# HGRN level scores: two chunks of tokens on one 128-column stationary tile

## The chip, the core and the metric

The kernel runs on one core of one Trainium2 chip. The metric is the device time of one execution, in microseconds. The engines meant below: TensorE (PE; PEld is its load of stationary operands), VectorE (DVE), ScalarE (ACT), GpSimd (POOL) and SyncE (SP), which issues most of the transfers. They run side by side, each through its own list of instructions in order, and wait for one another by semaphores.

## The reference

One decoder layer, float32, on 512 tokens of width 1024: a half-step SwiGLU FFN (hidden width 2816), a token mixer, and a second half-step FFN, each between two RMS norms. The mixer projects the normed input with one matrix and splits the columns among four HGRN2 heads (hq, hf, hi, hgate, 128 columns a head each) and four mLSTM heads. The change touches the HGRN2 heads:

```python
    """S_t = diag(f_t) S_{t-1} + k_t v_t^T (k_t = 1 - f_t), o_t = S_t^T q_t.
...
        G = jnp.cumsum(gc, axis=2)
        o_inter = jnp.einsum("bhtk,bhkv->bhtv", qc * jnp.exp(G), S)
        rel = G[:, :, :, None, :] - G[:, :, None, :, :]
        decay = jnp.exp(jnp.where(causal, rel, -jnp.inf))
        scores = jnp.sum(qc[:, :, :, None, :] * kc[:, :, None, :, :] * decay, axis=-1)
        o = o_inter + jnp.einsum("bhts,bhsv->bhtv", scores, vc)
```

The score of query t and key s (s not after t) is the sum over a head's 128 columns of q[t] k[s] exp(G[t] - G[s]), where G is the running sum of the logarithms of the forget gates. The exponent differs per column, so the factor cannot simply be split between q and k: exp(-G[s]) alone could overflow.

## The kernel before

**Stages.** The program does FFN1, then the mixer (about 340 to 600 us of the span), then FFN2. Weights come by SyncE (raw), are split by ScalarE (a rounded part, L294) and VectorE (the rest, L296) into two parts of a reduced format, and each projection is three matmuls of parts (L198 to L200 with the input as stationary operand, L549, L560 and L619 with the weight). Activations are split the same way into the tiles xq, one for each 256 tokens and 512 input columns: L370 on ScalarE and L371 on VectorE, behind transposes L364 on TensorE.

**Scores by levels.** Kernel chunks are 128 tokens, so there are 4 chunks and 16 pairs of head and chunk. Scores of a chunk are computed in seven levels, LEVELS = (1, 64, 32, 16, 8, 4, 2), and a diagonal. At level c the tokens are cut into blocks of 2c; queries of a block's second half meet keys of its first half, with the G at the end of the first half as reference, so both exponents are at most 0: qe = q exp(G - ref) on 64 queries of each chunk (L1421, L1423, L1428), and ke = exp(ref - kk), where kk holds G - ln k by then (L1422, L1424). Only first-half columns of a ke tile (128x2x512) are written, the others keep what they have; both ke tiles are first filled with a copy of kk (L1806). TensorE multiplies all columns up to the last used key: `rows(c)` is 72, 96, 112, 120, 124, 126 for c = 64 to 2. One matmul for each of the 8 pairs of a pass (a pass p is two heads) has these key columns stationary and 64 query columns moving (L1440). The result is (keys x queries), of which most pairs belong to no common block; a copy under a mask (L1445, `copy_predicated`, masks by L1314 and L1316 on GpSimd) puts the right ones into sT, the transposed scores. Level 1 is one matmul with ones (L1435); the diagonal is one of 128x128 by 128 for each head and chunk, L1486, copied under the mask eye (L1488). So in the kernel before

```python
            k8, q8 = flat(ke).rearrange("p (n s) -> p n s", s=P), qe.rearrange("p (n u) -> p n u", u=64)
            r = self.rows(c)
            for m in range(8):
                nc.tensor.matmul(sc[:r, 64 * m : 64 * m + 64], k8[:, m, :r], q8[:, m], start=True, stop=True)
```

The levels go two by two: `hgrn_levels` issues a pair's vector work, then `fill(n)`, n steps of projection matmuls from a list of jobs, and then the pair's matmuls in one group. There are three groups a pass, six in all. The jobs are hq, conv, rows, hi (the HGRN values, `job_t`, chunk of tokens stationary), mv (the mLSTM values, into vm), later hg and mo. `hgrn_decays` (L1374 to L1391) makes the decays of keys to the chunk's end (ek, L1389), which `hgrn_edges` transposes (L1401) into kdt for the state updates (L1498, with vh, the values of hi).

**Order.** The code is written in an order of dependence and filler steps, and a scheduler sorts each engine's instructions again before the program is built; which instruction stands where is therefore told below from the built programs. GpSimd makes the masks, then the sums f2sums over FFN2's output weights (L944, transfers that add, each waiting for the one before), then the memset of C (L1651) and the causal masks on the mLSTM's e (L1614). An mLSTM head's e comes from neg_m (L1588) over L1610 to L1614; L1624 multiplies it with the score of L1622 and frees their banks of PSUM. SyncE loads the gains of norms into two tiles of 1024 columns, gpre and gpost (L165), and graw, the weights of the gates' rows (L1515).

Of the kernel before, what the change touches and what calls it, by code (L numbers as in the profile page):

```python
# [8 lines left out]
F32 = mybir.dt.float32  # L9
# [114 lines left out]
class Layer:  # L124
# [1027 lines left out]
    def t_mm(self, ps, w, k, kk, i):  # L1152
        s = (i * P, (i + 1) * P)
        self.mm3(ps, self.xop(k, 0, *s), self.xop(k, 1, *s), w[:, 0, kk, :], w[:, 1, kk, :], k == 0, k == ND - 1)

    def job_t(self, name, then):

        acc = [self.ps() for _ in range(NT)]
        for k2 in range(ND // 2):
# [3 lines left out]
            for i in range(NT):  # L1163
                for kk in range(2):
                    self.t_mm(acc[i], w, 2 * k2 + kk, kk, i)
                    if kk == 0:
                        yield
# [137 lines left out]
    def masks(self, mc, mb):  # L1305
# [3 lines left out]
        self.mask = mb.tile([P, len(LEVELS), 64], I32, name="mask")  # L1309
        nc.gpsimd.memset(self.mask, 1)  # L1310
        for n, c in enumerate(LEVELS):
            m = self.mask[:, n, :].rearrange("p (b c) -> p b c", c=c)
            pat = [[-2 * c, 64 // c], [0, c]]
            nc.gpsimd.affine_select(m, m, pattern=pat, compare_op=ALU.is_ge, fill=0.0, base=0, channel_multiplier=1)  # L1314
            pat = [[2 * c, 64 // c], [0, c]]
            nc.gpsimd.affine_select(m, m, pattern=pat, compare_op=ALU.is_ge, fill=0.0, base=c - 1, channel_multiplier=-1)  # L1316
        self.eye = mb.tile([P, P], I32, name="eye")
        nc.gpsimd.memset(self.eye, 1)
        nc.gpsimd.affine_select(
            self.eye, self.eye, pattern=[[1, P]], compare_op=ALU.is_equal, fill=0.0, base=0, channel_multiplier=-1  # L1320
        )
# [51 lines left out]
    def hgrn_decays(self, p):  # L1373
# [15 lines left out]
        nc.vector.tensor_tensor(chunks(d), end.broadcast_to([P, 8, P]), chunks(H), op=ALU.subtract)  # L1389
# [14 lines left out]
    def rows(self, c):  # L1404

        return P if c == 1 else max(P - c, 72)

    def hgrn_level(self, p, n, ke):
# [4 lines left out]
        flat = lambda t: t.rearrange("p a t -> p (a t)")  # L1413
        blk = lambda t: flat(t).rearrange("p (b two c) -> p b two c", two=2, c=c)
        qe = self.st("qe")
        qe3 = qe.rearrange("p (b c) -> p b c", c=c)
        if c > 1:
            el = self.st("el")
            el3 = el.rearrange("p (b c) -> p b c", c=c)
            ref = blk(G)[:, :, 0, c - 1 : c].broadcast_to([P, 512 // c, c])  # L1420
            nc.vector.tensor_tensor(qe3, blk(G)[:, :, 1, :], ref, op=ALU.subtract)  # L1421
            nc.vector.tensor_tensor(el3, ref, blk(kk)[:, :, 0, :], op=ALU.subtract)  # L1422
            nc.scalar.activation(qe, qe, AF.Exp)  # L1423
            nc.scalar.activation(blk(ke)[:, :, 0, :], el3, AF.Exp)  # L1424
# [9 lines left out]
        if c == 1:  # L1434
            nc.tensor.matmul(sc, self.one.broadcast_to([P, P]), qe, start=True, stop=True)  # L1435
        else:
            k8, q8 = flat(ke).rearrange("p (n s) -> p n s", s=P), qe.rearrange("p (n u) -> p n u", u=64)
            r = self.rows(c)
            for m in range(8):
                nc.tensor.matmul(sc[:r, 64 * m : 64 * m + 64], k8[:, m, :r], q8[:, m], start=True, stop=True)  # L1440
        yield
        r = self.rows(c)
        so = self.sT[:, 8 * p : 8 * p + 8, :].rearrange("p n (b two c) -> p n b two c", two=2, c=c)[:, :, :, 1, :]
        mk = self.mask[:, n : n + 1, :].broadcast_to([P, 8, 64]).rearrange("p n (b c) -> p n b c", c=c)
        nc.vector.copy_predicated(so[:r], mk[:r], sc.rearrange("p (n b c) -> p n b c", n=8, c=c)[:r])  # L1445
# [34 lines left out]
    def hgrn_diag(self, p):  # L1480
        nc = self.nc
        for a in range(2):
            sc = self.ps()
            for c in range(NT):
                s = slice(c * P, (c + 1) * P)
                nc.tensor.matmul(sc[:, s], self.kk[p][:, a, s], self.q[p][:, a, s], start=True, stop=True)  # L1486
            h = 2 * p + a
            nc.vector.copy_predicated(  # L1488
                self.sT[:, 4 * h : 4 * h + 4, :], self.eye[:, None, :].broadcast_to([P, NT, P]), sc.rearrange("p (n s) -> p n s", s=P)
# [101 lines left out]
    def conv(self, n, ps):  # L1591
# [3 lines left out]
        nc.scalar.copy(x, ps)  # L1595
# [375 lines left out]
```

## Time and profile before

| | us |
|---|---|
| median of 3 runs | 928.69 |
| lowest and highest run | 927.12, 928.71 |
| profiled execution: its span | 926.8 |
| TensorE busy | 918.0 |
| VectorE, ScalarE, GpSimd busy | 765.4, 523.9, 184.0 |

The page gives no time of the profiled execution apart from its span, so the span stands for it. A row of a group gives line, engine, operation, output and inputs, shapes and count, then busy time and the mean of one in ns, then the idle time of the engine ahead of these instructions and who ended it. A row of the timeline gives start and length in us; instructions in sequence from one line are put together with their count, and an idle time ahead stands in brackets. A row of windows gives length, busy time and records of the engine, its granted clock, the transfer engines' share and rate. A matmul on plain float32 tiles leaves two records: the 8 of L1440 for one level and pass stand as 16.

### The profile page before, as it was taken

Reading aid. Unit: us, or ns where it says so; the run is one execution under the profiler, and the core shown is the slowest. Engines: PE = TensorE matmul, PEld = TensorE weight load, DVE = VectorE, ACT = ScalarE, POOL = GpSimd, SP = SyncE. Lnnn points to the kernel's source line nnn. Section 1 sums busy time; section 2 is a strip of 40 time slices with the busy share of each in tenths; the row PEclk is TensorE's granted clock in tenths of the full one; section 3 lists DMA queues with packets and bytes.
Section 4 is the critical chain, followed back from the end, with each engine's and each line's share of the span. In section 5 each row is a group of like instructions: output and inputs, shape, how many; then the busy total and the mean of one; then the engine's idle time right before and its main releaser. Section 6 shows DMA issues by size and latency. Waiting matters only on the chain.

```text
span 926.8 us, 18311 instructions
## 1 busy us (share of the span) xinstructions
PE 918.0 (99%) x7428; PEld 885.5 (96%) x7428; DVE 765.4 (83%) x993; ACT 523.9 (57%) x751; POOL 184.0 (20%) x252
## 2 busy tenths in 40 slices
PE   9999999999999999999999999999999999999997
PEld 8999999999999999998888887899999999999997
DVE  6899988889887877698757565799898989998886
ACT  7645455557566466956533345595454545756661
POOL 2531112111111045552230310314000000010002
PEclk9999999999999999999999999999999999999999
DMA  9354778766897925899742124352354435278542
GB/s 313 76 175 122 187 202 204 193 149 160 224 274 227 254 70 138 168 193 189 156 91 70 46 92 153 97 183 68 116 160 137 136 116 159 93 230 247 172 148 92
DMA packets 123384, 145.42 MB, mean 157 GB/s; under 512 B 12066, under 2 KB 96034, under 8 KB 123300
## 3 DMA queue, kind: packets, MB, share of 16 engines
q1 hardware_dynamic: 107332, 129.05, 45.7%
q0 software_dynamic: 15680, 14.69, 12.1%
q8 instruction: 58, 0.95, 0.4%
q10 hardware_dynamic: 288, 0.52, 0.2%
q14 instruction: 26, 0.21, 0.1%
HBM read 142.14 MB, written 31.46 MB: 187 GB/s over the span
## 4 chain that ended last, share of the span: by engine, by line
PE 63%; ACT 0%; DVE 0%; DVEq 0%; POOLq 0%; issue 0%; POOL 0%; ACTq 0%
PE ps L619 23%; PE ps L1012 8%; PE ps L549 6%; PE ps L198 5%; PE ps L200 5%; PE ps L199 5%; PE ps L1004 4%; PE ps L1440 2%; PE ps L560 1%; PE ps L364 1%; PE ps L1533 0%; PE ps L1738 0%; PE ps L1711 0%; PE ps L1486 0%; PE ps L1735 0%; PE ps L1498 0%
## 5 line engine op out<-in xcount | busy, mean ns | idle before, releaser
L294 ACT CAST w<-raw 128x1024 fp32r<-128x1024 f32 x246 | 250.9, 1028 | 196.1 <-PE ps L619 79.2
L296 DVE TENSOR_TENSOR w<-raw,w 128x1024 fp32r<-128x1024 f32 x246 | 299.2, 1220 | 31.2 <-ACT w L294 29.9
L619 PE MATMUL ps<-xq,w 128*128 128x256 f32 x2016 | 237.3, 277 | 0.0
L619 PEld LDWEIGHTS ps<-xq,w 128*128 128x128 f32 x2016 | 233.3, 188 | 0.0
L619 PE MATMUL ps<-sq,w 128*128 128x256 f32 x1512 | 178.4, 277 | 0.0
L619 PEld LDWEIGHTS ps<-sq,w 128*128 128x128 f32 x1512 | 174.9, 188 | 0.0
L310 DVE TENSOR_TENSOR raw<-raw,raw 128x1024 f32<-128x1024 f32 x72 | 89.7, 1250 | 7.7 <-DMA raw<-in_ffn_w_in_dram 6.4
L1012 PE MATMUL ps<-w,hs 128*128 128x256 f32 x672 | 80.9, 276 | 0.0
L1004 PE MATMUL ps<-w,hs 128*128 128x256 f32 x672 | 79.2, 276 | 0.0
L1012 PEld LDWEIGHTS ps<-w,hs 128*128 128x128 f32 x672 | 78.3, 188 | 0.0
L198 PE MATMUL ps<-w,xq 128*128 128x512 f32 x192 | 77.9, 407 | 0.1
L1004 PEld LDWEIGHTS ps<-w,hs 128*128 128x128 f32 x672 | 77.5, 188 | 0.0
L199 PE MATMUL ps<-w,xq 128*128 128x512 f32 x192 | 74.8, 391 | 0.0
L200 PE MATMUL ps<-w,xq 128*128 128x512 f32 x192 | 74.8, 391 | 0.0
L549 PE MATMUL ps<-xq,w 128*128 128x256 f32 x480 | 55.7, 277 | 0.0
L549 PEld LDWEIGHTS ps<-xq,w 128*128 128x128 f32 x480 | 54.9, 188 | 0.5 <-issue 0.5
L944 POOL DMA_DIRECT2D f2sums<-in_ffn_w_out_dram x15 | 20.2, 1492 | 176.4 <-DMA f2sums<-in_ffn_w_out_dram 176.1
L884 ACT CAST hs<-hf 128x1024 fp32r<-128x1024 f32 x32 | 33.7, 1053 | 28.0 <-PE ps L1012 20.3
L885 DVE TENSOR_TENSOR hs<-hf,hs 128x1024 fp32r<-128x1024 f32 x32 | 39.1, 1221 | 9.0 <-ACT hs L884 8.4
L944 POOL DMA_DIRECT2D f1sums<-f1sums x26 | 23.1, 889 | 106.3 <-DMA f1sums<-in_ffn_w_out_dram 55.4
L198 PEld LDWEIGHTS ps<-w,xq 128*128 128x128 f32 x192 | 36.1, 188 | 8.5 <-issue 1.0
L200 PEld LDWEIGHTS ps<-w,xq 128*128 128x128 f32 x192 | 36.0, 188 | 8.1 <-DVE xq L371 0.3
(272 smaller groups left out, 1216.8 us busy)
## 6 DMA issues: line engine op xcount, KB each, us to landing
raw<-in_ffn_w_in_dram SPq DMA_DIRECT2D x98, 512.0 KB, 4.6
raw<-in_ffn_w_out_dram SPq DMA_DIRECT2D x44, 512.0 KB, 4.8
raw<-in_w_mix_in_dram SPq DMA_DIRECT2D x28, 512.0 KB, 6.8
raw<-f2sums SPq DMA_DIRECT2D x15, 512.0 KB, 4.4
raw<-f1sums SPq DMA_DIRECT2D x13, 512.0 KB, 6.0
raw<-in_w_mix_out_dram SPq DMA_DIRECT2D x8, 512.0 KB, 3.8
f2sums<-in_ffn_w_out_dram SPq DMA_DIRECT2D x30, 128.0 KB, 5.2
f2sums<-in_ffn_w_out_dram SPq DMA_DIRECT2D x15, 256.0 KB, 5.7
```

Of the source, the lines that this page charges most:

```text
L198: mm(ps, sh, mh, start=start, stop=False, **kw)
L199: mm(ps, sh, ml, start=False, stop=False, **kw)
L200: mm(ps, sl, mh, start=False, stop=stop, **kw)
L294: nc.scalar.copy(hi, raw)
L296: self.low = nc.vector.tensor_tensor(lo, raw, hi.bitcast(F32), op=ALU.subtract)
L310: added = (nc.vector if late else nc.gpsimd).tensor_tensor(o, o, c, op=ALU.add)
L549: mm(ps[:, u0:u1], w[:, a, k, :], self.xop(k, b, u0, u1), start=k + n + m == 0, stop=k == ND - 1 and n == 2, skip_group_check=True,)
L619: self.nc.tensor.matmul(ps[:, c], wb[b][:, k, v], left[d][:, k, :], start=first and a + n + k == 0, stop=n == 2 and k == KH - 1, skip_grou ...
L885: self.nc.vector.tensor_tensor(lo, src, hi.bitcast(F32), op=ALU.subtract)
L944: nc.gpsimd.dma_start(to[:, a:b], v, accum_op=ALU.add)
L1004: mm(out, a[kk][:, i * P : (i + 1) * P], w[:, b, kk, QUARTER * v : QUARTER * (v + 1)], start=begin and c == kk == n == 0, stop=kk == 1 and ...
L1012: mm(ps[:, QUARTER * c : QUARTER * (c + 1)], A[a][:, c], B[b], start=begin and c == n == 0, stop=n == 2, skip_group_check=True,)
```

## The change

Keys of two neighbouring chunks are put on one stationary tile. At each level the even chunk's used keys lie in first halves of blocks; the odd chunk's tokens are written in reversed order, so that its first halves fall on the columns of the second halves. Both together fill 128 columns, none unused. One matmul has these 128 columns stationary and the 64 queries of both chunks, 128 columns, moving; a pass has 4 of them at a level instead of 8. Its result has four blocks (even or odd keys by even or odd queries), of which the mask takes two. The rows of odd chunks in sT then stand in reversed token order, and everything that is contracted with them too: the diagonal's keys (new copies kr on ScalarE, L1495 of the changed program), ek, and the HGRN values, which `hi` computes from a reversed copy of the input (`turned_x`, four ScalarE copies of 128x1024, L1161). The copies for the first 256 tokens take the tiles of gpre and gpost, so that the gains for the mixer's output are loaded later; those for the other 256 take the place of vm, which is made only when mv begins. The mask and eye get a second half for odd chunks (28 selects instead of 14). The subtractions for el and ek are split into an even and an odd one. The copies L1806 are gone.

```diff
-    def job_t(self, name, then):
+    def turned_x(self, c, h):
+
+        t = self.cp.tile([P, D], F32R, tag=("gpre", "gpost")[h], bufs=1, name=self.nm("xr")) if c == 0 else self.xr1[:, h, :]
+        self.xr[c, h] = t.rearrange("p (b k t) -> p b k t", b=2, t=P)
+        self.nc.scalar.copy(self.xr[c, h], self.xq[2 * c + h][:, :, :, : P - 1 : -1].bitcast(F32))
+
+    def job_t(self, name, then, *order):
...
-            m = self.mask[:, n, :].rearrange("p (b c) -> p b c", c=c)
...
+            for odd in range(2):
+                m = self.mask[:, n, odd, :].rearrange("p (b c) -> p b c", c=c)
+                for sign, base in ((1, 0), (-1, c - 1)):
...
-        nc.vector.tensor_tensor(chunks(d), end.broadcast_to([P, 8, P]), chunks(H), op=ALU.subtract)
+        for odd, out in enumerate((parity(chunks(d))[:, :, 0], parity(chunks(d))[:, :, 1, ::-1])):
+            e, h = (parity(t)[:, :, odd] for t in (end, chunks(H)))
+            nc.vector.tensor_tensor(out, e.broadcast_to([P, 4, P]), h, op=ALU.subtract)
...
-            nc.vector.tensor_tensor(el3, ref, blk(kk)[:, :, 0, :], op=ALU.subtract)
+            el = self.st("el").rearrange("p (m s) -> p m s", s=P)
+            for odd in range(2):
+                halves = lambda t: t.rearrange("p m (b two c) -> p m b two c", two=2, c=c)[:, :, :, 0, :]
+                chunk = lambda t: halves(t.rearrange("p a (c o s) -> p (a c) o s", o=2, s=P)[:, :, odd, :])
+                g = chunk(G)
+                nc.vector.tensor_tensor(
+                    halves(el[:, :, ::-1] if odd else el), g[:, :, :, c - 1 : c].broadcast_to(g.shape), chunk(kk), op=ALU.subtract
+                )
             nc.scalar.activation(qe, qe, AF.Exp)
-            nc.scalar.activation(blk(ke)[:, :, 0, :], el3, AF.Exp)
+            nc.scalar.activation(ke, el, AF.Exp)
...
-            r = self.rows(c)
-            for m in range(8):
-                nc.tensor.matmul(sc[:r, 64 * m : 64 * m + 64], k8[:, m, :r], q8[:, m], start=True, stop=True)
+            for m in range(NT):
+                v = slice(m * P, (m + 1) * P)
+                nc.tensor.matmul(sc[:, v], ke[:, m, :], qe[:, v], start=True, stop=True)
...
+        kr = self.st("kr").rearrange("p (a n s) -> p a n s", a=2, n=2)
+        nc.scalar.copy(kr, self.kk[p].rearrange("p a (n o s) -> p a n o s", o=2, s=P)[:, :, :, 1, ::-1])
...
+                k = kr[:, a, c // 2, :] if c % 2 else self.kk[p][:, a, s]
+                nc.tensor.matmul(sc[:, s], k, self.q[p][:, a, s], start=True, stop=True)
...
+                self.jobs.append(self.job_t("hi", lambda i, ps: nc.scalar.copy(self.vh[:, i].rearrange("p h v -> p (h v)"), ps), self.xr))
+                self.jobs.append(self.job_t("mv", lambda i, ps: self.values_mv(ma, i, ps)))
...
-                for ke in kes:
-                    nc.scalar.copy(ke, self.kk[0])
...
-                    nc.gpsimd.memset(self.vm[:, :, :, P : P + 1], 1.0)
...
+    def values_mv(self, ma, i, ps):
+        if i == 0:
+            self.vm = ma.tile([P, NT, NH, 129], F32, tag="vm", bufs=1, name="vm")
+            self.nc.gpsimd.memset(self.vm[:, :, :, P : P + 1], 1.0)
```

Three places of the built programs follow; in a row, the output stands left of the arrow, and a number behind a name tells versions of a tile apart.

TensorE, the third group of the first pass (levels 4 and 2), before:

```order
L200 MATMUL ps_5195<-w,xq_78 128x512
L1440 MATMUL ps_5254<-qe_5178,ke_4366 124x64 x8
L1440 MATMUL ps_5263<-qe_5185,ke_4365 126x64 x8
L198 MATMUL ps_5196<-w,xq_76 128x512
L199 MATMUL ps_5196<-w,xq_76 128x512
```

and now:

```order
L200 MATMUL ps_5206<-w,xr_4876 128x512
L1451 MATMUL ps_5265<-qe_5187,ke_4365 128x128 x4
L1451 MATMUL ps_5270<-qe_5195,ke_4364 128x128 x4
L198 MATMUL ps_5207<-w,xq_76 128x512
L199 MATMUL ps_5207<-w,xq_76 128x512
```

The group stands at the same place among hi's matmuls, with 8 matmuls instead of 16; the matmul of an odd chunk ahead of it reads the reversed input.

ScalarE at the start of the mixer, where the second 256 tokens are split (xq_76 and xq_77) and the weights of the first projections come:

```order
 L294 CAST w<-raw_3832 128x1024
 L453 ACTIVATE junk_4189,col_4187<-xs 128x512
+L1161 CAST xr_4952<-xq_75 128x1024
 L453 ACTIVATE junk_4194,col_4192<-xs 128x512
 L294 CAST w<-raw_4201 128x1024
 L370 CAST xq_76<-ps_4270 128x4x128
 L370 CAST xq_77<-ps_4277 128x4x128
+L1161 CAST xr_4876<-xq_78 128x1024
 L370 CAST xq_76<-ps_4308 128x4x128
 L370 CAST xq_77<-ps_4315 128x4x128
+L1161 CAST xr_4368<-xq_76 128x1024
+L1161 CAST xr_4368<-xq_77 128x1024
```

All four reversed copies stand here, one ahead of a square sum L453 and one ahead of the last L370.

GpSimd at the end of its sums, before the mLSTM scores, before the change:

```order
L944 DMA f2sums_8_107<-in_ffn_w_out_dram 128x2x256
L944 DMA f2sums_8_107<-f2sums_8_107 128x256 x2
L1651 MEMSET C 128x1548
L1614 AFFINE_SELECT e_5679<-e_5679 128x512
L1614 AFFINE_SELECT e_5687<-e_5687 128x512
```

and now:

```order
L944 DMA f2sums_8_107<-in_ffn_w_out_dram 128x2x256
L944 DMA f2sums_8_107<-f2sums_8_107 128x256 x2
L1850 MEMSET vm 128x16
L1669 MEMSET C 128x1548
L1632 AFFINE_SELECT e_5669<-e_5669 128x512
```

The ones of vm came from ahead of the sums (behind the masks) to behind them; the sums themselves are issued in the order of before.

More of the change, by code (lines that the diff above doesn't have):

```diff
@@ L1150, in job_f, with t_mm @@
         yield
-    def t_mm(self, ps, w, k, kk, i):
+    def t_mm(self, ps, w, k, kk, i, turned=None):
         s = (i * P, (i + 1) * P)
-        self.mm3(ps, self.xop(k, 0, *s), self.xop(k, 1, *s), w[:, 0, kk, :], w[:, 1, kk, :], k == 0, k == ND - 1)
-    def job_t(self, name, then):
+        xh, xl = (turned[i // 2, k // KH][:, b, k % KH, :] if turned and i % 2 else self.xop(k, b, *s) for b in range(2))
+        self.mm3(ps, xh, xl, w[:, 0, kk, :], w[:, 1, kk, :], k == 0, k == ND - 1)
+    def turned_x(self, c, h):
[3 more added lines that the diff above has]
+    def job_t(self, name, then, *order):
         acc = [self.ps() for _ in range(NT)]
@@ L1485, in hgrn_diag @@
                 s = slice(c * P, (c + 1) * P)
[L1486 removed]
+                k = kr[:, a, c // 2, :] if c % 2 else self.kk[p][:, a, s]
+                nc.tensor.matmul(sc[:, s], k, self.q[p][:, a, s], start=True, stop=True)
             h = 2 * p + a
+            two = lambda t: t.rearrange("p (n o s) -> p n (o s)", o=2, s=P)
             nc.vector.copy_predicated(
[L1489 removed]
+                two(self.sT[:, 4 * h : 4 * h + 4, :].rearrange("p n s -> p (n s)")),
+                self.eye.rearrange("p o s -> p (o s)")[:, None, :].broadcast_to([P, 2, 2 * P]), two(sc),
             )
```

49 lines of the change are left out of this document (22 added, 27 removed).

## The prediction

> **What bounds the kernel now.** I read the summary of the page first, then TensorE's waits.
>
> ```profile
> span 926.8 us, 18311 instructions
> PE 918.0 (99%) x7428; PEld 885.5 (96%) x7428; DVE 765.4 (83%) x993; ACT 523.9 (57%) x751; POOL 184.0 (20%) x252
> PE ps L194 <- POOL ones L172: 1.2, 1, 1.2
> PE ps L364 <- DVE xn L754: 0.5, 1, 0.5
> PE ps L619 <- ACT xq L384: 0.2, 1, 0.2
> ```
>
> TensorE is busy for 918.0 of 926.8 us, and in the whole span it waited 1.9 us for anything, 1.2 of them at the start. So the time is the length of TensorE's instruction stream. Work elsewhere counts only if it makes TensorE wait; a microsecond taken out of the stream is gained whole, as long as every other engine can follow that much earlier. The question is therefore what the score matmuls cost in the stream. A matmul's own duration does not tell it, since neighbours overlap; I took each group's stretch from its first start to the start of the matmul behind it, and put the groups side by side in the view of windows: six level groups (two levels each, L1440), then two diagonal groups (L1486).
>
> ```profile
> core 0: us, PE busy (x), PEclk, DMA share, GB/s
> 403.57:405.96 2.39, 2.39 (x34) 1.00 1.20 206
> 415.85:419.03 3.18, 3.18 (x35) 1.00 0.95 304
> 427.32:430.74 3.42, 3.42 (x33) 1.00 0.85 212
> 451.32:453.71 2.39, 2.39 (x34) 1.00 0.83 127
> 461.99:465.17 3.18, 3.18 (x34) 1.00 0.86 178
> 472.11:475.55 3.44, 3.44 (x34) 1.00 0.91 121
> 384.51:386.21 1.70, 1.70 (x19) 1.00 1.09 133
> 435.67:437.37 1.70, 1.70 (x17) 1.00 1.06 93
> L1440 PE MATMUL ps<-qe,ke 128*126 128x64 f32 x32 | 3.8, 273 | 0.0
> L1440 PE MATMUL ps<-qe,ke 128*72 128x64 f32 x32 | 2.4, 227 | 0.0
> L1486 PE MATMUL ps<-q,kk 128*128 128x128 f32 x32 | 3.9, 275 | 0.0
> ```
>
> The groups of forms say what is in a window: each level shape (stationary x moving, here 128\*126 by 64) has 32 records for the two passes over head pairs, 16 a pass; the program has 8 matmuls a level and pass, so a float32 matmul leaves two records. A level group is 32 records. It takes 2.39 us with 72 and 96 stationary columns, 3.18 with 112 and 120, 3.42 and 3.44 with 124 and 126: the cost per record goes with the stationary columns (75 ns at a mean of 84, 107 ns at 125). A diagonal group is 16 records, 128 stationary columns and 128 moving ones, in 1.70 us: 106 ns per record, no more than a record with 125 stationary columns and half the moving ones. The granted clock is 1.00 in all eight rows.
>
> **The term on TensorE.** The six groups take 2.39 + 3.18 + 3.42 + 2.39 + 3.18 + 3.44 = 18.00 us. After the change a level has 4 matmuls of 128 stationary and 128 moving columns, the exact shape of L1486, so a group is 16 records. By that row it costs 1.70 us; if the cost per stationary column of the 124/126 groups (107/125 ns) is carried to 128 columns, 16 x 0.1096 = 1.75. If loads did not matter and only moving columns did (four times 128 instead of eight times 64, the same number), nothing would be gained; the 72/96 groups against the 124/126 groups speak against it, as both move 64 columns. I take 1.70: six groups are 10.20 us, and the stream gets **7.80 us** shorter (7.5 at 1.75). The number of other matmuls and their shapes stay; the diagonal keeps its shape with another stationary source.
>
> The Trainium skill, "TensorE: Matmul & The Clock Gate", section "LDWEIGHTS (loading the stationary operand)", says that a load takes its columns divided by 1.2 in ns: 107 ns for 128, an estimate beside the 106 measured here, and the trace agrees.
>
> **What is added on ScalarE, at the hand-over.** Prices for whole copies come from this view of groups.
>
> ```profile
> L1806 ACT COPY ke<-kk 128x1024 f32<-128x1024 f32 x2 | 2.1, 1046 | 0.0
> L1595 ACT COPY cx<-ps 128x512 f32<-128x512 f32 x4 | 2.3, 574 | 0.0
> L1424 ACT ACTIVATE ke<-el 128x512 f32<-128x512 f32 x12 | 7.7, 638 | 3.4 <-PE ps L1440 2.1 <-DVE el L1422 1.3
> L1423 ACT ACTIVATE qe<-qe 128x512 f32<-128x512 f32 x12 | 7.6, 632 | 7.3 <-DVE qe L1421 7.1
> ```
>
> Four reversed copies of the normalized input (128x1024) come in, two kr copies (128x512) too, and the two ke copies L1806 go: 4 x 1.05 + 2 x 0.57 - 2 x 1.05 = +3.2 us. No row reads backwards. L1424 writes short pieces with gaps and takes 638 ns beside 632 for the gapless L1423, so an irregular step costs nothing in the nearest row; a gain has no ground in it, and from above I can only bound it by what it would do (the last rival). I take 1.05. Two of the four copies stand where it is tight, between the two halves of the mixer's input:
>
> ```profile
> 342.95 0.63 ACT L453 ACTIVATE junk<-xs 128x512 f32<-128x512 f32 x1
> 343.99 1.78 POOL L454 TENSOR_SCALAR col<-col,col 128x1 f32<-128x1 f32 x1
> 346.44 1.41 DVE L481 SCALAR_TENSOR_TENSOR hf<-xs,col,gpre 128x512 f32<-128x512 f32 x2 [0.80 <-POOL col L458]
> 348.89 1.08 ACT L370 CAST xq<-ps 128x512 fp32r<-128x512 f32 x2 [2.38 <-PE ps L364]
> 348.91 2.48 DVE L371 TENSOR_TENSOR xq<-ps,xq 128x512 fp32r<-128x512 f32 x4
> 351.87 4.36 PE L549 MATMUL ps<-xq,w 128*128 128x256 f32 x37
> 349.48 0.53 SPq L1515 DMA_DIRECT2D graw<-in_w_mix_in_dram  x1
> 354.67 1.05 ACT L294 CAST w<-raw 128x1024 fp32r<-128x1024 f32 x1 [4.70 <-PE ps L549]
> ```
>
> The first copy stands ahead of the L453 at 342.95, whose sums go through GpSimd to L481, the transposes and the xq that L549 at 351.87 reads. L453 starts 1.05 later at most. GpSimd's L454 behind it took 1.78 us, by far the longest of its small steps, and may be shorter when it comes later; xq is ready at 351.39 (348.91 + 2.48), 0.48 ahead of its reader. So TensorE loses 1.05 - 0.48 = 0.57 us at most, and nothing if L454 is shorter; I take 0.1. The second copy waits for L481's end at 347.85 and is over at 348.90, when L370 at 348.89 starts. The third and fourth fit the idle 4.70 us ahead of 354.67 (349.97 to 354.67). That cover is gone only if a copy takes more than 2.3 us. A kr copy of 0.57 stands where a ke copy of 1.05 stood, ahead of the diagonal matmuls, and so delays nothing.
>
> **VectorE.** The change splits each el subtraction L1422 (678 ns) into two halves and each of the two ek subtractions likewise; the score copies (L1445) keep their 512 elements a partition.
>
> ```profile
> L1422 DVE TENSOR_TENSOR el<-G,kk 128x512 f32<-128x512 f32 x12 | 8.1, 678 | 0.0
> L501 DVE TENSOR_TENSOR hf<-ps,gpost 128x256 f32<-128x256 f32 x16 | 6.2, 414 | 0.9 <-ACT junk L453 0.9
> 423.29 1.29 DVE L1428 TENSOR_TENSOR qe<-qe,q 128x512 f32<-128x512 f32 x2
> ```
>
> A half costs 0.41 by L501, so a level costs 2 x 0.41 - 0.68 = +0.15 and twelve cost 1.8; the two for ek, split in the same way, get the same 0.15 each. The tightest place is the third group of the first pass: TensorE now comes there 0.69 + 1.48 us earlier, at 427.32 - 2.17 = 425.15, and at its second level 0.85 later, 426.0. That level's qe is the last of the two L1428 that end at 424.58; six levels' halves ahead of it make that 424.58 + 0.9 = 425.5. Slack 0.5 us: VectorE hides its extra work, and if a reversed write cost a half 0.1 us more, TensorE would lose about 0.1 there. I take 0 to 0.5, and 0.1.
>
> **GpSimd.** The fourteen mask selects become twenty-eight, and the ones of vm are set behind the sums over FFN2's weights (f2sums).
>
> ```profile
> L1316 POOL TENSOR_SCALAR_AFFINE_SELECT mask<-mask 128x64 int32<-128x64 int32 x7 | 4.3, 632 | 0.0
> L1314 POOL TENSOR_SCALAR_AFFINE_SELECT mask<-mask 128x64 int32<-128x64 int32 x7 | 3.5, 516 | 0.0
> 374.12 0.73 POOL L1324 MEMSET sel<- 4x768 f32 x1 [6.74 <-DVE G L1366]
> 480.40 0.81 POOL L944 DMA_DIRECT2D f2sums<-f2sums  x1 [2.84 <-DMA f2sums<-f2sums]
> 481.26 1.40 POOL L1651 MEMSET C<- 128x1548 f32 x1
> 484.89 0.83 POOL L1614 TENSOR_SCALAR_AFFINE_SELECT e<-e 128x512 f32<-128x512 f32 x1 [2.24 <-ACT e L1613]
> 489.54 1.29 DVE L1624 SCALAR_TENSOR_TENSOR pT<-ps,e 128x512 f32<-128x512 f32 x2
> 494.58 0.48 PE L1588 MATMUL ps<-nm,selr 36*128 36x512 f32 x1
> ```
>
> The masks add 4.3 + 3.5 = 7.8 us and the second eye about 0.5 (estimate from these). 6.7 of it lies in GpSimd's own wait ahead of 374.12, so its sums start 0 to 1.6 us later. The sums are a chain of issues that wait for transfers; their last stands at 480.40, and two memsets later GpSimd waits only 2.24 us for the e that it masks. TensorE, 7.8 us earlier, wants e masked at 477.1. If the chain stays where it is, the first select comes at 482.7 instead, and L1624 (planned at 481.7) after two selects at 484.5. The next TensorE instruction that needs a score bank of L1624 is L1588, at 486.8; the first L1624 is done at about 485.1. That leaves 1.6 us, so nothing is lost until the chain is 1.6 us later than now. I take 0.
>
> **SyncE.** The gain loads (gpost, gpre) were issued ahead of graw at 349.48; their buffers now hold reversed input, so they are issued later, among the weight loads of hi's and mv's stretch. graw moves ahead, which helps GpSimd's start. The weight load behind each gain waits for a buffer that TensorE frees at about the same place of its stream, and no wait of TensorE on a weight stands in its list above, so I cost the move at nothing; the other end is a gain that shares the transfers with the sums and delays them, the first rival.
>
> **Sum.** 926.8 - 7.80 + 0.1 + 0.1 = 919.2 us of span. The three runs have their median at 928.69, 1.9 over the profiled span, and the lowest 0.3 over it: 919.5 to 921.1, and **921.0** by the median. The likeliest case's own range is 919.3 (no loss, by the lowest run) to 922.3 (7.5 gained, 0.6 and 0.5 lost, by the median).
>
> **The rivals.** (1) *GpSimd's sums become the bound* for a while. For it: their chain now ends 2.24 us ahead of need and 7.8 us of work is put in front, with two gain loads to share the transfers. Against it: part of what the chain waits for are loads that SyncE issues (L938 to L940) between weight loads, and those come earlier when TensorE does. Chain late by 4 us: TensorE waits 4 - 1.6 = 2.4 us at L1588, 923.4 us. (2) *Nothing is gained*, because the moving columns bind: 928.7. The Trainium skill, "FP8 and Floating Point Precision", section "TensorE Precision Notes", has true FP32 at four passes through the array, which by column counts alone would give the same before and after; the 2.39 against 3.44 us of groups with equal moving columns is against it. A smaller form: a reversed source slows the matmul's load, but ke and kr are written reversed and read straight, so only the copies see it. (3) *Slower:* a copy that reads backwards costs several times 1.05 us. The first one then delays L453 and all behind it, and the second delays L370 of the other half, each by its excess c - 1.05, and TensorE has nothing else to run ahead of 351.87. Both together eat the gain from 2(c - 1.05) = 7.8 on, at c = 5 us; at six times the row, 6.3 us, the loss is 10.5 and the time 928.7 - 7.8 + 10.5 = 931.4. Only the unshown direction speaks for it; the row of gapped writes (L1424) speaks against any such factor.
>
> **How the numbers follow.** Likeliest 0.78, GpSimd 0.13, no gain 0.05, slower 0.04. What a measurement of this kernel can tell from no change is 0.2%, 1.9 us, so faster means under 926.8: the first two cases, less a little for their mixtures with costs not seen, 0.88. Within 0.2% 0.06, slower 0.06. The range 919.0 to 924.8 takes in the likeliest's own, and the GpSimd case with 1.4 us more of delay than priced.
>
> **What would show it.** Right: the six groups of score matmuls 1.70 us each, 16 records of 128\*128 by 128; TensorE's waits still near 2 us; the reversed copies 1.05 us and L549 of the second half without idle ahead; halves of el 0.41 us; sums that end near 480 and the selects on e behind them with no idle. Wrong: groups over 2.5 us (rival 2), idle on TensorE named for score banks or VectorE's pT near 480 to 490 (rival 1), copies of 3 us and more with an idle TensorE near 350 (rival 3), or lost time outside the mixer, where instructions stay in order.

## The result, and the profile after

| | kernel before | changed kernel |
|---|---|---|
| median of 4 runs, us | 928.05 | 920.51 |
| lowest to highest, us | 927.12 to 928.71 | 919.16 to 920.77 |
| profiled span, us | 926.8 | 918.9 |

The change makes the kernel faster by 0.8% (ratio 0.992, interval 0.9908 to 0.9932). On the page of the changed kernel TensorE's lines are some 8 us shorter; VectorE, ScalarE and GpSimd are busy 2.7, 0.3 and 6.6 us longer. Of TensorE's waits, the last row is new:

```profile
span 918.9 us, 18150 instructions
PE 910.2 (99%) x7332; PEld 877.3 (95%) x7332; DVE 768.1 (84%) x1007; ACT 524.2 (57%) x753; POOL 190.6 (21%) x267
...
PE ps L198 <- DVE sT L1457: 0.2, 1, 0.2
```

TensorE is as full as it was. The 0.2 us on L1457, the masked copy of scores, is the only new wait. ScalarE's busy time grew by only 0.3 us, though the copies add some 3.3, mainly because its list has 24 table loads of 1.28 us each where it had 26. The windows of the six level groups of the changed kernel, each again from its first start to the start of the next matmul (length, TensorE busy, records, granted clock):

```profile
404.23:406.01 1.78, 1.78 (x18) 1.00 1.10 196
415.88:417.58 1.70, 1.70 (x18) 1.00 1.07 336
425.99:427.69 1.70, 1.70 (x17) 1.00 0.64 127
448.41:450.19 1.78, 1.78 (x17) 1.00 1.08 183
458.68:460.38 1.70, 1.70 (x18) 1.00 1.17 192
467.30:469.08 1.78, 1.78 (x18) 1.00 0.84 152
sum 10.44, PE 10.44; mean PE 1.74
```

They take 10.44 us where the old groups took 18.00: 7.56 us less, nearly the whole difference of the medians, 7.54. The three groups of 1.78 are those with another plain float32 matmul behind them (transposes or state updates).

To see where the rest of the 7.9 us of span lies, take two points that both programs have, L549 at the hand-over (351.87 before) and the first matmul of FFN2. Changed kernel first, then the kernel before:

```profile
352.53 3.68 PE L549 MATMUL ps<-xq,w 128*128 128x256 f32 x31
...
590.77 2.98 PE L619 MATMUL ps<-xq,sq 128*128 128x256 f32 x24
```

```profile
597.29 2.99 PE L619 MATMUL ps<-xq,sq 128*128 128x256 f32 x24
```

FFN1 and the hand-over end 0.66 us later, the mixer is 245.42 - 238.24 = 7.18 us shorter, and FFN2 takes 328.13 instead of 329.51, 1.38 less. FFN1 and FFN2 have the same instructions in both, so 0.66 and 1.38 are differences between two executions (e5 and e7 below, with the same FFN1, reach the hand-over at 351.73 and 351.26). The mixer's 7.18 is the 7.56 less 0.4 of small losses, of which the wait above is a part.

Two rows of the groups of the changed kernel show the added work, the reversed copy (L1161) and the half of el (L1432), and three of GpSimd's timeline the sums and the causal select on e (L1632):

```profile
L1161 ACT CAST xr<-xq 128x1024 fp32r<-128x1024 f32 x4 | 4.1, 1044 | 2.4 <-DVE hf L481 1.6 <-DVE xq L371 0.9
L1432 DVE TENSOR_TENSOR el<-G,kk 128x256 f32<-128x256 f32 x24 | 9.2, 416 | 0.0
```

```profile
380.06 4.32 POOL L944 DMA_DIRECT2D f2sums<-in_ffn_w_out_dram  x4
...
476.33 0.81 POOL L944 DMA_DIRECT2D f2sums<-f2sums  x1 [2.79 <-PE ps L200]
...
479.65 0.82 POOL L1632 TENSOR_SCALAR_AFFINE_SELECT e<-e 128x512 f32<-128x512 f32 x1 [1.02 <-ACT e L1631]
```

A reversed copy takes 1044 ns, the same as the forward one of before (1046). The first one delays the square sum L453, but nothing behind it: GpSimd's L454, which took 1.78 us before, now takes 1.18, and L481 stands 5.42 us ahead of L549 where it stood 5.43:

```profile
345.27 1.18 POOL L454 TENSOR_SCALAR col<-col,col 128x1 f32<-128x1 f32 x1 [0.70 <-ACT junk L453]
```

The sums f2sums start at 380.06 (before 379.74) in spite of twice the masks, and end at 476.33, 4.07 us earlier than before. The first select on e still has to wait for ScalarE, so GpSimd holds nothing up.

### The profile page after: what moved, and what is told of

Read it like the earlier page. It is cut to its first block, busy times and chain, and to the rows that moved or that the text cites. A ratio compares the mean times of both kernels' runs of the same rounds, so it can differ in the third digit from the quotient of the medians.

```text
span 918.9 us, 18150 instructions
## 1 busy us (share of the span) xinstructions
PE 910.2 (99%) x7332; PEld 877.3 (95%) x7332; DVE 768.1 (84%) x1007; ACT 524.2 (57%) x753; POOL 190.6 (21%) x267
## 4 chain that ended last, share of the span: by engine, by line
PE 57%; DVE 3%; ACT 2%; DMA 1%; issue 1%; SPq 0%; DVEq 0%; POOLq 0%; POOL 0%; ACTq 0%
PE ps L619 23%; PE ps L1012 8%; PE ps L549 5%; PE ps L1004 4%; PE ps L198 4%; PE ps L200 4%; PE ps L199 4%; PE ps L560 1%; PE ps L364 1%; DMA f2sums<-in_ffn_w_out_dram 1%; PE ps L1756 0%; PE ps L1451 0%; PE ps L1729 0%; DVE w L296 0%; DVE sT L1457 0%
## 5 line engine op out<-in xcount | busy, mean ns | idle before, releaser
L296 DVE TENSOR_TENSOR w<-raw,w 128x1024 fp32r<-128x1024 f32 x246 | 299.8, 1222 | 30.2 <-ACT w L294 28.8
L198 PE MATMUL ps<-w,xq 128*128 128x512 f32 x176 | 71.6, 408 | 0.2 <-DVE sT L1457 0.2
L199 PE MATMUL ps<-w,xq 128*128 128x512 f32 x176 | 68.6, 391 | 0.0
L200 PE MATMUL ps<-w,xq 128*128 128x512 f32 x176 | 68.6, 391 | 0.0
L549 PE MATMUL ps<-xq,w 128*128 128x256 f32 x480 | 55.7, 277 | 0.0
L549 PEld LDWEIGHTS ps<-xq,w 128*128 128x128 f32 x480 | 54.9, 188 | 0.5 <-issue 0.5
L884 ACT CAST hs<-hf 128x1024 fp32r<-128x1024 f32 x32 | 33.7, 1053 | 28.0 <-PE ps L1012 20.3
L944 POOL DMA_DIRECT2D f2sums<-f2sums x30 | 26.1, 897 | 84.0 <-DMA f2sums<-in_ffn_w_out_dram 40.2
L310 POOL TENSOR_TENSOR raw<-raw,raw 128x1024 f32<-128x1024 f32 x12 | 32.6, 2721 | 40.9 <-DVE w L296 40.7
```

The costliest lines, as they stand in the source:

```text
L198: mm(ps, sh, mh, start=start, stop=False, **kw)
L199: mm(ps, sh, ml, start=False, stop=False, **kw)
L200: mm(ps, sl, mh, start=False, stop=stop, **kw)
L296: self.low = nc.vector.tensor_tensor(lo, raw, hi.bitcast(F32), op=ALU.subtract)
L310: added = (nc.vector if late else nc.gpsimd).tensor_tensor(o, o, c, op=ALU.add)
L549: mm(ps[:, u0:u1], w[:, a, k, :], self.xop(k, b, u0, u1), start=k + n + m == 0, stop=k == ND - 1 and n == 2, skip_group_check=True,)
```

## The experiments

All start from the changed kernel. What was asked: what sets the price of a level group (e1, e2, e3, e9, e10); how near the three engines that take the added work are to making TensorE wait (e4 to e7); and whether the other small score matmuls can be made cheaper in turn (e8, with e11 and e12, which its result called for).

**e1: the pairing undone on TensorE alone.**

```diff
-                nc.tensor.matmul(sc[:, v], ke[:, m, :], qe[:, v], start=True, stop=True)
+                for o in range(2):
+                    u = slice(m * P + 64 * o, m * P + 64 * o + 64)
+                    nc.tensor.matmul(sc[:, u], ke[:, m, :], qe[:, u], start=True, stop=True)
```

> The changed kernel with one part undone: every level's stationary tile still holds the used keys of two chunks on 128 columns, but the 64 queries of each chunk go in a matmul of their own, so a level has 8 matmuls of 128 columns by 64 again. Reversed copies, masks, split subtractions and the order of SyncE's loads stay. Theory (a record costs what its stationary columns take to load): 32 records of 107 ns, 3.42 us a group instead of 1.70, 6 x 1.72 = 10.3 us more TensorE time; span 918.9 + 10.3 = 929.2, that is 0.2 to 0.4% slower than the kernel before. Rival (the streamed columns bind, and the gain came from something else in the change): the streamed columns are those of the changed kernel, so groups stay near 1.7 and the time near 920.5.

Measured: 931.48, ratio to the kernel before 1.0043 (1.0028 to 1.0059), span 929.0. The first and last group:

```profile
403.12:406.64 3.52, 3.52 (x35) 1.00 1.11 266
...
474.83:478.34 3.51, 3.51 (x33) 1.00 0.50 90
sum 21.01, PE 21.01; mean PE 3.50
```

The groups cost 21.01 instead of 10.44, 10.6 us, and the span is 10.1 longer. So the number of stationary tiles loaded makes the gain, and not the streamed columns, the reversal, the order of the gain loads or anything else that came with it. Of the 4.1 us that e1 is over the kernel before, 3.0 are its wider tiles: 128 columns in every group against 72 to 126 (21.01 against 18.00).

**e2, e3: half the queries, half the keys.**

```diff
-                nc.tensor.matmul(sc[:, v], ke[:, m, :], qe[:, v], start=True, stop=True)
+                u = slice(m * P, m * P + 64)
+                nc.tensor.matmul(sc[:, u], ke[:, m, :], qe[:, u], start=True, stop=True)
...
+                nc.tensor.matmul(sc[:64, v], ke[:, m, :64], qe[:, v], start=True, stop=True)
```

> The changed kernel with only the even chunks' 64 queries moving in each level matmul (128 stationary columns by 64 moving); the scores of odd chunks' queries at the levels are left out, and the masked copies are half as long. If the load of the stationary operand alone sets the price: groups stay at 1.70 us and the span at 918.9 within 0.5. If the moving columns alone set it: 16 records of 53 ns, 0.85 us a group, span 913.8. If load and stream both take about 107 ns at 128 by 128 and overlap: 1.70 and 918.9, as under the first; the next run tells these two apart.

> The changed kernel with only the first 64 stationary columns in each level matmul (64 by 128 moving); the keys on the other 64 columns are left out of the level scores, and the masked copies take 64 partitions. If the load alone sets the price: at 0.86 to 0.89 ns a column (from the groups of before, 107 ns at 125 and 75 at 84) 55 to 57 ns a record, 0.9 us a group, span 914.1. If the moving columns alone set it, or if load and stream each take about 107 ns and overlap: groups stay at 1.70 and the span at 918.9.

A group of e2 and one of e3:

```profile
415.07:416.77 1.70, 1.70 (x18) 1.00 1.04 283
```

```profile
415.41:417.30 1.89, 1.89 (x17) 1.00 1.05 299
```

Half the stream saves nothing, 1.70; the six groups of e2 take 10.20 us against 10.44. Half the load saves nothing either and is dearer: all six groups of e3 take 1.89, where they took 1.70 or 1.78, which none of the expectations had. Spans are 917.9 and 919.6 (medians 919.47 and 921.89). Of the 1.0 us by which e2's span is shorter than that of the changed kernel, 0.78 lie ahead of the hand-over, in FFN1.

**e9, e10: the whole range of sizes.** Six widths each, one for each group:

```diff
+                r = ((32, 64, 96), (112, 120, 124))[p][(n - 1) // 2]
+                nc.tensor.matmul(sc[:r, v], ke[:, m, :r], qe[:, v], start=True, stop=True)
...
+                u = ((16, 32, 64), (80, 96, 112))[p][(n - 1) // 2]
+                nc.tensor.matmul(sc[:, m * P : m * P + u], ke[:, m, :], qe[:, m * P : m * P + u], start=True, stop=True)
```

> The changed kernel with 32, 64, 96 stationary columns in the three level groups of the first pass and 112, 120, 124 in those of the second, always with 128 moving columns (the keys on the other columns are left out of the level scores). Known: 128 columns 1.70 us a group, 64 columns 1.89 (118 ns a record). If a record costs the longer of load and stream: all six 1.70, and the 1.89 was something else. If a tile that leaves columns unused costs 0.19 more whatever its width: 1.89 in all six. If the extra grows with the unused columns: 32 above 1.89, 96 between 1.70 and 1.89, 124 at 1.70. In every case no narrower tile is cheaper than 128 columns by 128.

> The changed kernel with 128 stationary columns and 16, 32, 64 moving columns in the level groups of the first pass and 80, 96, 112 in those of the second (the other queries are left out of the level scores; VectorE first sets the score tile to zero, 12 small operations more). Known: 64 and 128 moving columns 1.70 us a group. If a record costs the longer of load and stream: all six 1.70. If some of the stream adds to the load: below 1.70 for 16 and 32.

e9, with 32, 64, 96, 112, 120 and 124 stationary columns in this order:

```profile
403.74:405.60 1.86, 1.86 (x17) 1.00 1.14 189
415.81:417.70 1.89, 1.89 (x17) 1.00 1.09 291
426.11:427.77 1.66, 1.66 (x17) 1.00 0.23 58
448.48:450.23 1.75, 1.75 (x18) 1.00 1.07 153
458.54:460.21 1.67, 1.67 (x18) 1.00 1.17 201
467.11:468.86 1.75, 1.75 (x18) 1.00 0.82 109
```

In the same places the changed kernel has 1.78, 1.70, 1.70, 1.78, 1.70 and 1.78. So 32 and 64 columns cost 0.08 and 0.19 more than 128, and 96 to 124 cost 0.03 or 0.04 less; none of the three expectations holds for all six.

e10, with 16 moving columns (a whole group), 32 (half a group), and 96 (a whole group):

```profile
402.88:404.58 1.70, 1.70 (x18) 1.00 1.15 222
414.69:415.50 0.81, 0.81 (x11) 1.00 1.01 375
...
465.87:467.57 1.70, 1.70 (x18) 1.00 1.06 306
```

With 128 moving columns no narrower tile saves more than 0.04 us. With 128 stationary columns a group costs 1.70 whether 16 or 96 columns move, and 1.62 with 32 or 64, in two halves of 0.81 with other work between (112 columns took 1.77, with state updates behind; the group with 80 ran at a halved clock and is not read).

Where the stream is short, the load shows by itself. Level by level, from first start to next start, the kernel before took 1.03, 1.36, 1.53, 1.65 and 1.68 us for 72, 96, 112, 120 and 124 stationary columns with 64 moving ones: 64, 85, 96, 103 and 105 ns a record. Where the stream is long, it shows by itself: level 1, with 512 moving columns, takes 0.43 us a record, four times 0.107. Together this reads: a record costs the longer of its load and its stream, and at 128 by 128 both take about 106 ns. The pairing filled the stationary tile and doubled the stream of each matmul up to the point where the stream takes as long as the load. Why 32 and 64 stationary columns cost more than 128 stays open.

e9 took 920.58 us in its one execution. e10 took 929.58, which is no price of its groups: the zeroing that it adds on VectorE made TensorE wait 2.7 us ahead of the fourth group, and the granted clock was 0.50 for some 10 us behind that.

By the Trainium skill, "TensorE: Matmul & The Clock Gate", section "LDWEIGHTS (loading the stationary operand)", a load of 72 columns is an estimated 60 ns and one of 64 columns 53. The trace agrees within a tenth where the stream is short, with 64 ns a record at 72 columns; e3, with 64 columns and 128 moving ones, shows 118.

**e4: GpSimd's selects twice.**

```diff
+                    for again in range(2):
                         nc.gpsimd.affine_select(m, m, pattern=pat, compare_op=ALU.is_ge, fill=0.0, base=base, channel_multiplier=step)
```

> The changed kernel with every mask select on GpSimd made twice (56 instead of 28; the result is the same), about 15.6 us more ahead of the sums over FFN2's weights, which then start near 395 instead of 380. Theory now (the sums are paced by loads that SyncE issues between weight loads, so the chain catches up): its last issue stays within 1 us of 476.3, TensorE's waits stay under 1 us, the time stays at 920.5 within 1. Rival of the prediction (the chain only moves as a whole): last issue near 490, the masked e near 492, TensorE waits 14.6 - 1.0 - 1.6 = 12 us near 480 to 490, 932.

Measured: 930.28, ratio 1.0034 (1.0016 to 1.0052), span 929.6; its ten runs lie between 927.38 and 933.64. GpSimd's first and last sum and the first select on e, then TensorE's wait, then windows of TensorE's clock:

```profile
394.02 4.32 POOL L944 DMA_DIRECT2D f2sums<-in_ffn_w_out_dram  x4
...
491.86 0.81 POOL L944 DMA_DIRECT2D f2sums<-f2sums  x1 [2.79 <-DMA f2sums<-f2sums]
...
494.11 2.41 POOL L1633 TENSOR_SCALAR_AFFINE_SELECT e<-e 128x512 f32<-128x512 f32 x4
```

```profile
PE ps L1606 <- DVE pT L1643: 7.1, 1, 7.1
```

```profile
496.00:500.00 4.00, 4.00 (x12) 0.50 0.29 81
500.00:504.00 4.00, 4.00 (x15) 0.72 0.14 52
504.00:508.00 4.00, 4.00 (x20) 1.00 0.32 92
```

The theory that I had formed from the result, that the sums catch up, fell: the chain starts 13.96 us later and ends 15.53 later, so it moves as a whole, as the prediction's first rival had it. That rival's place was right too: L1606 waits for pT. Its slack was not: the select comes 14.46 us late and TensorE waits 7.05, so 7.4 us were to spare, and not 1.6. And the wait has a tail: the clock is halved for about 6 us after it, which costs an estimated 3 more of the 10.7 us of span.

**e5, e6: the reversed copies twice and five times** (e6 has a 5 where e5 has this 2).

```diff
+        for again in range(2):
             self.nc.scalar.copy(self.xr[c, h], self.xq[2 * c + h][:, :, :, : P - 1 : -1].bitcast(F32))
```

> The changed kernel with each of the four reversed copies of the input made twice: 4.2 us more on ScalarE at the hand-over. In its list one extra copy stands ahead of the first two L370 and one directly ahead of the last two. By the prediction's pricing (the excess of both copies goes to TensorE, 2 x 1.05, less 0.48 of slack): L549 of the second half 1.6 us later behind its predecessor, 922.1. By the trace of the changed kernel (the extra copy ahead of the first L370 delays nothing that is waited for; the last L370 ends 1.05 later, xq is ready at about 352.3 of 352.53): 0 to 0.3, 920.5 to 920.8.

> The same with each copy made five times, about 16.6 us more on ScalarE between 343 and 375 us, spread by the scheduler: one ahead of the first L370, three between the first and the last two, the rest among the weights' splits of the next 15 us. By the prediction's pricing of a slow copy (c = 5.2 us: 2 x 4.15 - 0.48): 7.8 us lost, 928.3. If ScalarE's later work has the room (weights are split several matmul groups ahead of use): about 1 us at L549, since the last L370 ends near 352.7 and L371 near 353.4, and nothing later: 921.5 to 922.5.

Measured: e5 919.75, ratio 0.9918 (0.9903 to 0.9932), no slower than the changed kernel; e6 926.87, ratio 0.9989 (0.998 to 0.9999). The hand-over of e6 (L371 makes the second part of the last xq, L549 reads it), and e6's longer waits:

```profile
351.24 1.29 DVE L371 TENSOR_TENSOR xq<-ps,xq 128x512 fp32r<-128x512 f32 x2 [1.16 <-ACT xq L370]
```

```profile
348.93 2.98 PE L560 MATMUL ps<-xq,w 128*128 128x256 f32 x24
351.75 1.44 PE L549 MATMUL ps<-xq,w 128*128 128x256 f32 x9
```

```profile
PE ps L198 <- DVE sT L1458: 1.9, 1, 1.9
...
PE ps L1452 <- ACT cx L1613: 1.1, 1, 1.1
PE ps L1452 <- ACT ke L1437: 0.8, 1, 0.8
PE ps L1452 <- DVE qe L1441: 0.7, 1, 0.7
```

L549 follows L560 without a gap in both, even with three copies in a row ahead of the last L370. The pricing of the prediction was too pessimistic there: in e6 the two L371 end at 352.53, 0.78 us after L549 has begun, and it does not wait. The times fit a reading in which the first of the two tiles is the one that L549 needs first, so that the 0.48 us that I took from the end of both is not the slack; the program agrees, since L549 goes through the input columns in order and the second tile holds the upper half of them. The other path, over L453, is not tested: in both runs the scheduler left one copy ahead of it, as in the changed kernel. In e6 the loss is real, 6.4 us, but it arises 55 to 105 us later, where the level groups wait for ScalarE's and VectorE's results. So e6 comes within 1.5 us of the first expectation's number, for a reason that neither had.

**e7: the el subtractions twice.**

```diff
-            for odd in range(2):
+            for odd in (0, 1, 0, 1):
                 halves = lambda t: ...
```

> The changed kernel with every half of the el subtraction made twice (the same result): 24 x 0.416 = 10 us more on VectorE, 5 us of it ahead of the third level group of the first pass. Theory (VectorE is in one stretch of work there with 0.5 us to spare, of which the changed kernel already shows 0.2 of waiting): TensorE waits 4 to 5 us in all near 405 to 430, 924.5 to 925.5. Rival (VectorE, 84% busy, has room): under 1 us, 920.5 to 921.5.

Measured: 923.01, ratio 0.9952 (0.9938 to 0.9967), span 920.5; 2.5 us slower than the changed kernel, under the theory and over the rival.

```profile
PE ps L198 <- ACT kdt L1414: 1.6, 1, 1.6
...
PE ps L1451 <- ACT ke L1436: 0.4, 1, 0.4
...
PE ps L1451 <- DVE qe L1440: 0.2, 1, 0.2
```

Ten microseconds more on VectorE cost TensorE 2.2 us of waits. At the third group of the first pass it is 0.2 us, where 5 us of added work had 0.5 to hide in by my reckoning. The scheduler had put other VectorE work behind it there (a weight split L296 and the product for level 1 of the next pass), so the slack is larger than the gap in a list that was ordered for other work. The gap itself was larger too: in the changed kernel this qe is ready at 424.95 and its first matmul starts at 426.88, 1.9 us later.

**e8: level 1 and the diagonal as sums with ones in the reduced format.**

```diff
+        parts = [self.sp.tile([P, 512], F32R, tag="st", bufs=4, name=self.nm("oh")) for _ in range(2)]
+        self.two_parts(*parts, t)
...
+            self.nc.tensor.matmul(sc, self.one_r.broadcast_to([P, P]), v, start=n == 0, stop=n == 1)
...
+            nc.vector.tensor_tensor(t, self.kk[p][:, a], self.q[p][:, a], op=ALU.mult)
...
+        self.one_r = mc.tile([P, 1], F32R, name="one_r")
```

> The changed kernel with level 1 and the diagonal done as column sums: the products q k are made on VectorE (new for the diagonal), split into two parts of the reduced format (ScalarE, VectorE), and summed by matmuls with a stationary tile of ones, 2 of 128x512 for each 512 columns. TensorE by rows: a 512-column record in the reduced format takes 0.228 us, a plain float32 matmul of 512 columns 0.86, a diagonal group 1.70 a pass: 2 x (0.86 - 0.46) + 2 x (1.70 - 0.91) = 2.4 us less. Work added: VectorE 4 x 0.69 + 6 x 0.68 = 6.8, half of it ahead of the first pass's tight place; ScalarE 6 x 0.57 - 2 x 0.62 = 2.2. If VectorE hides it: 918.1. If its 3.4 us come through at the third group: 3.1 lost, 921.2. TensorE 2.4 us earlier also uses up most of the 2.6 us that GpSimd's sums have left.

Measured: 948.91, ratio 1.0232 (1.0217 to 1.0247), span 947.7: far outside what was expected. TensorE waits for the new casts (L884), and the clock falls behind that:

```profile
PE ps L1503 <- ACT oh L884: 7.3, 2, 6.1
PE ps L1503 <- DVE oh L885: 1.5, 1, 1.5
...
400.00:404.00 4.00, 4.00 (x18) 0.50 0.99 114
```

Waits and clock account for some 12 of the 28 us over the changed kernel. Some 13 more lay in FFN1 and FFN2, where nothing had changed. Hence two controls:

**e11, e12: where the tiles lie.** e11 is e8 with the new constant of 64 bytes a partition in place of 4; e12 is the changed kernel with one more small constant.

```diff
-        self.one_r = mc.tile([P, 1], F32R, name="one_r")
+        self.one_r = mc.tile([P, 16], F32R, name="one_r")[:, :1]
...
+        nc.vector.tensor_copy(mc.tile([P, 1], F32, name="four"), self.one)
```

> The run of level 1 and the diagonal as sums with ones was 28 us slower than the changed kernel, but only some 13 of it stand at waits and a halved clock in the mixer; in its FFN1 and FFN2, which it does not touch, 20 us hold 171 records of TensorE instead of 178 at a granted clock of 1.00. It has one more constant tile, of 4 bytes a partition, which moves the weight tiles that are allocated behind it by 32 bytes. Here the same kernel with that tile made 64 bytes, so that those tiles move by 64. If the 32 bytes cost it: 178 records in 20 us of FFN2 again, 13 to 15 us faster than that run, 934 to 936, still slower than the kernel before, since ScalarE's new casts stay where TensorE waits 6 us for them. If the slower matmuls come from something else in that kernel: near 949 again.

> The changed kernel with nothing but one more constant tile of 4 bytes a partition (one small VectorE copy at the start), which moves the tiles allocated behind it by 32 bytes. If the place of the tiles sets the matmuls' pace: 171 records in 20 us of FFN2, hand-over 6 us later, 932 to 935. If not: 920.5, as the changed kernel.

Measured: e11 955.92, ratio 1.0307 (1.0293 to 1.0321); e12 938.56, ratio 1.0119 (1.0105 to 1.0133). The same 50 us of FFN1 in the changed kernel, e12 and e11, where the number in brackets is the records that TensorE did:

```profile
200.00:250.00 50.00, 50.00 (x443) 1.00 0.65 163
```

```profile
200.00:250.00 50.00, 50.00 (x435) 1.00 0.63 155
```

```profile
200.00:250.00 50.00, 50.00 (x429) 1.00 0.60 148
```

A constant that nobody reads costs 18 us, more than the 932 to 935 expected: FFN1 is 6.2 us longer, the mixer 4.6 and FFN2 7.2. With the tiles behind it 32 bytes further on, a record of FFN1 takes 114.9 ns instead of 112.9; 64 bytes further on, 116.6. In FFN1 TensorE, ScalarE and VectorE execute the same instructions in the same order in all three, and the clock is 1.00, so it is the place. Why, and which of the moved tiles matters, these runs do not tell; that 64 bytes would restore the pace was wrong. The kernels before and after place their weight tiles alike, and both do 443 records in this stretch, as do e1 to e7, e9 and e10, which add no tile. The fair comparison for e8 is e12: 948.91 - 938.56 = 10.4 us slower, about what the waits (7.3 + 1.5 + 0.7 on VectorE's qe) and some 3 us of halved clock come to, less the 2.4 gained. No version that computes the whole result beat the changed kernel clear of the noise.

## Why the prediction was right, point by point

- **The term on TensorE** (18.00 - 10.20 = 7.80): measured 18.00 - 10.44 = 7.56. The row that priced it, the diagonal group of the same shape, held; the 0.08 at each of three group ends was not in it. e1 undoes this term alone and takes 10.1 us more of span.
- **The first end of its bound** (load or stream): I took the load to be what binds. At the new shape load and stream bind alike (e2, e9, e10), so the term was right, and that half the moving columns cost no less is true only up to 128; with 512 a record takes 0.43 us.
- **Reversed copies** at 1.05 us: 1.044. The 0.1 us set down for the hand-over was nothing (L549 directly behind L560). The condition named for that held: L454 got shorter, from 1.78 to 1.18 us. The 0.48 us of slack was too small for a copy ahead of L370 (e5, e6), so the third rival's break-even of 5 us a copy was too low at that place; for the copy ahead of L453 no run tells.
- **VectorE**: halves 0.416 against 0.41. The third group showed no wait; the new wait of 0.2 us is on a masked copy in the second pass, near 451.8, a place that I had not priced. The slack of 0.5 was too small: 1.9 in the changed kernel, and more where the scheduler could reorder (e7).
- **GpSimd**: twice the masks moved the sums' start by 0.32 us, inside the 0 to 1.6. That the chain's end would stay at 480.40 was wrong: it came to 476.33, though it started no earlier. Its length is not fixed: 100.7 us before, 96.3 after, 97.8 in e4; what sets it is not shown. The slack of 1.6, counted from 480.40, was too small even so: e4's chain starts its last sum at 491.86 and TensorE waits 7.05 us, so one at 484.81 would have cost nothing, 4.4 us after 480.40. Of the 2.8 us that were missing, 1.3 are that TensorE came 6.5 us earlier there and not 7.8; the rest fits the first select sufficing where I had put two. The mechanism of that rival is real, as e4 shows, and its price left out the halved clock behind the wait.
- **SyncE's moved gains** at nothing: no wait of TensorE on a weight or gain appears.
- **Sum**: 919.2 of span against 918.9, 921.0 against 920.51. The mechanism carried it, but the closeness owes something to luck: FFN1 and FFN2 differed by +0.66 and -1.38 between the two executions, and the 0.4 us that the mixer lost stands against the 0.2 priced, none of it at the two places that were priced.

## What to carry to other kernels

When an engine is full and others have room, price an edit by the stretch from start to next start of a row that already has the new shape; for plain float32 matmuls that stretch here was the longer of load and stream (32 and 64 stationary columns apart), so filling the stationary tile pays until the stream takes as long. A gap in another engine's list is not its slack: follow which tile is read first, and what else could be moved, before a bound is put on it. And keep the place of tiles fixed when versions are compared, since one constant of 4 bytes cost more here than twice what the change gained.

## What the runs showed of the hardware that I had not expected

- A stall of TensorE costs more than its length. After 7.05 us of waiting (e4) the granted clock was 0.50 for about 6 us, after 6.09 (e8) likewise. A short one can be enough: in e6 a wait of 1.86 us was followed by 0.50 for some 3 us, and in e10 one of 2.72 by some 10 us, while 1.57 in e7 was not. The rows of e6 and e7 behind their waits, and one of e10 8 us behind its wait:

```profile
456.00:458.00 2.00, 1.75 (x5) 0.64 0.88 258
458.00:460.00 2.00, 2.00 (x7) 0.50 0.56 70
```

```profile
456.00:460.00 4.00, 4.00 (x20) 1.00 0.53 55
```

```profile
460.00:462.00 2.00, 2.00 (x6) 0.50 0.84 121
```

  The Trainium skill, "TensorE: Matmul & The Clock Gate", section "What's actually happening", has the clock fall after an idle window of about 3.4 us; e4 and e8 agree, e6 and e10 fell after a shorter one.
- The pace of TensorE's matmuls hangs on where tiles lie in memory: 112.9, 114.9 and 116.6 ns a record at shifts of 0, 32 and 64 bytes, at a clock of 1.00 (e12, e11).
- A narrower stationary tile can be dearer: at the same stream and in the same places, a group with 32 or 64 columns took 0.08 or 0.19 us more than one with 128, and one with 96 to 124 took 0.03 or 0.04 less (e9).
